# Moving eight modulation blocks into the output projection, and reading and projecting one branch's operands by token chunks

## The chip, the cores and the metric

The kernel runs on one core of a Trainium2 chip. A core has a matmul engine (TensorE, PE in the profile), a vector engine (VectorE, DVE), an activation engine (ScalarE, ACT), a general engine (GpSimd, POOL) and an engine that mostly issues transfers (SyncE, SP). Each engine takes its own instructions strictly in order; engines wait for one another through semaphores. 16 DMA engines move data between the large memory (HBM) and the on-chip memory. Matmuls write into accumulation banks (PSUM), which VectorE and ScalarE read. The metric is the device time of one execution in microseconds, lower is better.

## What is computed

One layer of a hybrid encoder in fp32, for 1024 prompt tokens and 64 sample tokens (2 sequences in all, D_MODEL = 1024). Both sequences share the weights and are laid side by side, 1088 tokens. Cut to what matters here:

```python
mod = jax.nn.silu(c) @ w_ada + b_ada                  # 6 x 1024 numbers for each sequence
sh1, sc1, g1, sh2, sc2, g2 = jnp.split(mod[:, None, :], 6, axis=-1)
u = _rmsnorm(x, norm1_g) * (1 + sc1) + sh1
proj = u @ w_in                                       # q, k, v, mLSTM operands, gates ga and gb
...
y_a = _stick_breaking(q, k, v)                        # scores, log-sigmoids, reverse cumsum, product with v
...
y_b = jax.nn.sigmoid(mo) * h                          # mLSTM branch
merged = jax.nn.sigmoid(ga) * (y_a @ w_a) + jax.nn.sigmoid(gb) * (y_b @ w_b)
x = x + g1 * (merged @ w_out)
u2 = _rmsnorm(x, norm2_g) * (1 + sc2) + sh2
x = x + g2 * ((silu(u2 @ w_ff_gate) * (u2 @ w_ff_up)) @ w_ff_down)
```

`g2` is the last of the six modulation vectors. Nothing reads it before the down projection of the feed-forward part.

## The kernel before

**Number format and tiles.** A matrix product in fp32 is made of three matmuls on pairs of reduced-precision parts, a high part and the rest (`mm3`, L76 to L78: high x high, high x low, low x high). Weight tiles come as a raw tile (`wr`, 512 KB, three buffers), which is turned into a high and a low part (`wh`, `wl`, three buffers each) by `w_unit` (L61); its load is L64. POOL makes these parts by default (L53 the high, L59 the low part), ACT and VectorE where the call says so (L47 and L56). D_MODEL is cut into 8 blocks of 128 (`KB` = 8). The 1088 tokens are cut into chunks of 320, 384 and 384 (`CHUNKS`), in the output projection into four quarters of 272. Long-lived activations are tiles of 128 x 1088 in a pool `up` of 16 slots: during the input projection these hold the normalised input (`uh0` to `uh7`, `ul0` to `ul7`), afterwards other tiles take the slots as they come free.

**What sets the order.** The program is written as generators that are drawn in turns (`run`, `chain`), and a scheduler of the compiler then fixes one order of instructions for each engine, by its own estimates of durations. On the chip nothing is reordered.

**Modulation blocks.** `ada_blocks` (L213) makes one block of 128 of the 6144 modulation numbers: a load of 512 KB of `w_ada` (L220), matmuls with the few columns of `c` (L223), a copy from the bank to the small tile `ada_sb` by VectorE (L226), a transpose on PE (L228), a sum and an addition of the bias. There are 48 blocks; blocks 40 to 47 are `g2`. Blocks 16 to 47 (`ada_left`) are filler, nearly all of them in the attention phase.

**The attention phase.** Four head pairs, `attention(0)` to `attention(3)`, each for two heads in turn. For each key tile: scores (`z`, L526 and L527), a mask, exponentials on ACT, a scan along the keys on VectorE (L396), a product (`be`, L397), transposes of that product on PE (named `ps_a<-ident,be`, L540), high and low parts (`ah` by ACT, `al` by VectorE, L56), and products with the values (`po`, L547). Matmuls of other work are put between, since the attention alone is a chain through four engines. In pairs 0 to 2 this filler is the gate units of the input projection (`gate_unit`, the last one `gb7`) and modulation blocks. In pair 3 it is the last eight modulation blocks and then `branch_b`.

**Branch b.** The mLSTM result has been put aside in HBM as ready high and low parts (`yb_d`). `load_y(4..7)` reads them into eight tiles `yh4` to `yh7`, `yl4` to `yl7` (L968), 544 KB each, into slots of the input tiles. `branch_b` then makes 8 output blocks `m` x 3 chunks `c`, chunks innermost, 12 matmuls each (`ps_b`). For each such unit the sigmoid gate `lgb` is read from HBM (L995), the sums are copied by ACT to `tb` (L997), multiplied by the gate on POOL (L998) and stored to `pb_d` (L999). `lgb` and `tb` share four small buffers. Between them `load_y(0..2)` reads three of the four stored attention outputs (`yr`, L971) and POOL makes their parts `yh0` to `yh2`, `yl0` to `yl2` (L53, L59); the fourth comes from pair 3 itself.

**Branch a and the output projection.** Branch a takes `yh0` to `yh3` through `w_a` (also named `ps_a`, now `ps_a<-yh`, L76), is gated, and added to branch b's result. Then the output projection's first half: for each `m` in 0 to 7, `wo_weights(m)` loads and converts `w_out`'s block (`wr_wo`, `wh_wo`, `wl_wo`) and reads the residual input (`xs`, 64 rows, through three buffers of the tag `dg`; `xr`), and `wo_half(m, 0)` makes two quarters with 24 matmuls each (`ps_wo`), with nine transposes of the residual input (`ps_xt`, L1105) into banks of `sbank`.

## Time and profile before

| | |
|---|---|
| three runs, us | 1793.95, 1791.36, 1785.57 (median 1791.36) |
| the profiled execution | 1789.02 us, of which 1787.1 us lie between its first and last instruction (the span) |
| mean granted clock of TensorE | 0.985 of full speed |
| busy: PE / VectorE / ScalarE / POOL | 1719.9 / 1050.1 / 741.3 / 547.1 us |
| the stretch that the change rewrites | 784.6 (end of `gb7`) to 899.1 us (first matmul of branch a) |
| the output projection's first half | from about 949 to 1003 us |

Times in all views are counted from the first instruction. A "busy" window says how long an engine had an instruction in work; the granted clock says which share of full speed the chip let TensorE have. A wait is shown in square brackets as the idle time of an engine just before an instruction, with the instruction of another engine (or the DMA) that ended it.

### The profile page before, as it was taken

How to read it: one execution, taken by the hardware profiler on the slowest of the kernel's cores; microseconds unless marked ns; L12 is line 12 of the kernel's file. 1: busy time of each engine (PE TensorE's matmuls, PEld its weight loads, DVE VectorE, ACT ScalarE, POOL GpSimd, SP SyncE). 2: the span in 40 equal slices, each digit the busy share in tenths (PEclk: the TensorE clock that was granted, in tenths of full speed). 3: DMA queues.
4: the chain of work that ended last, by engine and by line, in shares of the span. 5: the costliest groups of instructions: out<-in, count | busy, mean ns of one | idle time of the engine just before them, and what ended most of it. 6: DMA issues, size and time to landing. Idle time of an engine off the chain costs nothing. (4 is left out here: it accounts for less than half of the span.)

```text
span 1787.1 us, 32780 instructions
## 1 busy us (share of the span) xinstructions
PE 1719.9 (96%) x12670; PEld 1658.1 (93%) x12670; DVE 1050.1 (59%) x2030; ACT 741.3 (41%) x1506; POOL 547.1 (31%) x495
## 2 busy tenths in 40 slices
PE   5999999999999999988899999999999999999998
PEld 4799999999989988877899999999999999999998
DVE  6633415142346858696644289666555677667964
ACT  5333333324334535453523457433333355453444
POOL 2434544545343232224657250044322100001000
PEclk8999999999999999998999999999999999999999
DMA  9426566664386566586576345644433488899943
GB/s 269 123 64 212 129 218 138 197 162 141 122 213 144 142 147 156 137 245 195 179 231 202 99 141 161 196 158 148 144 108 98 147 243 236 290 343 340 295 151 101
DMA packets 359534, 320.25 MB, mean 179 GB/s; under 512 B 16727, under 2 KB 327507, under 8 KB 359379
## 3 DMA queue, kind: packets, MB, share of 16 engines
q1 hardware_dynamic: 345074, 270.77, 50.5%
q0 software_dynamic: 14304, 47.39, 10.7%
q8 instruction: 100, 1.64, 0.4%
q14 instruction: 56, 0.45, 0.1%
HBM read 241.01 MB, written 98.09 MB: 190 GB/s over the span
## 5 line engine op out<-in xcount | busy, mean ns | idle before, releaser
L1619 PE MATMUL ps_d<-o,wh_d 128*128 128x272 f32 x1232 | 230.8, 287 | 0.0
L1619 PEld LDWEIGHTS ps_d<-o,wh_d 128*128 128x128 f32 x1232 | 192.8, 188 | 0.0
L1619 PE MATMUL ps_d<-o,wl_d 128*128 128x272 f32 x616 | 176.4, 288 | 0.0
L1619 PEld LDWEIGHTS ps_d<-o,wl_d 128*128 128x128 f32 x616 | 115.5, 188 | 0.0
L47 ACT CAST w<-wr 128x512 fp32r<-128x512 f32 x140 | 85.0, 619 | 67.5 <-PE ps_gc L1392 22.0
L396 DVE TENSOR_TENSOR_SCAN re<-re 128x128 f32<-128x128 f32 (+3 forms) x64 | 103.3, 1615 | 14.8 <-ACT re L392 14.4
L56 DVE TENSOR_TENSOR w<-wr,w 128x512 fp32r<-128x512 f32 x140 | 94.6, 688 | 21.4 <-ACT w L47 19.2
L1603 POOL DMA_DIRECT2D dsum_d<-wr_d x12 | 6.5, 540 | 237.7 <-DVE wr_d L1601 221.2
L392 ACT ACTIVATE re<-z 128x512 f32<-128x512 f32 (+2 forms) x96 | 47.5, 495 | 72.7 <-DVE z L388 54.2
L1392 PE MATMUL ps_ga<-b1h,w 128*128 128x272 f32 x352 | 74.6, 289 | 3.0 <-ACT g L1377 1.8
L1392 PE MATMUL ps_gc<-b5h,w 128*128 128x272 f32 x352 | 75.2, 293 | 0.0
L1392 PE MATMUL ps_gd<-b7h,w 128*128 128x272 f32 x352 | 74.2, 290 | 0.2 <-DVE hst L1384 0.2
L1392 PE MATMUL ps_gb<-b6h,w 128*128 128x272 f32 x352 | 74.3, 289 | 0.0
L1392 PE MATMUL ps_gd<-b4h,w 128*128 128x272 f32 x352 | 74.0, 290 | 0.3 <-DVE hst L1374 0.2
L1392 PE MATMUL ps_gc<-b3h,w 128*128 128x272 f32 x352 | 73.7, 289 | 0.0
L1392 PE MATMUL ps_ga<-b2h,w 128*128 128x272 f32 x352 | 73.7, 288 | 0.0
L47 ACT CAST o<-hr 128x544 fp32r<-128x544 f32 x77 | 48.9, 645 | 51.0 <-DMA hr<-h_d 27.3
L47 ACT CAST wh_d<-wr_d 128x1024 fp32r<-128x1024 f32 (+1 forms) x42 | 41.1, 980 | 67.6 <-PE ps_d L1619 31.9
L76 PE MATMUL ps_ga<-uh,wh_ga 128*128 128x384 f32 (+1 forms) x192 | 64.6, 336 | 3.5 <-ACT gt_ga L825 3.4
L56 DVE TENSOR_TENSOR o<-hr,o 128x544 fp32r<-128x544 f32 x77 | 53.8, 720 | 20.7 <-ACT o L47 20.4
L56 DVE TENSOR_TENSOR al<-ps_a,ah 128x512 fp32r<-128x512 f32 (+1 forms) x80 | 49.5, 631 | 25.8 <-ACT ah L47 25.4
L76 PE MATMUL ps_gb<-uh,wh_gb 128*128 128x384 f32 (+1 forms) x192 | 64.6, 336 | 0.0
(552 smaller groups left out, 5884.8 us busy)
## 6 DMA issues: line engine op xcount, KB each, us to landing
wada<-in_w_ada SPq DMA_DIRECT2D x48, 512.0 KB
wr<-wsum_d SPq DMA_DIRECT2D x80, 256.0 KB
wr_d<-in_w_ff_down SPq DMA_DIRECT2D x34, 512.0 KB
h_d<-hst SPq DMA_DIRECT2D x44, 272.0 KB
wr<-in_w_ff_gate SPq DMA_DIRECT2D x40, 256.0 KB
hr<-h_d SPq DMA_DIRECT2D x33, 272.0 KB
wsum_d<-in_w_ff_up POOLq DMA_DIRECT2D x6, 1282.0 KB, 7.7
wsum_d<-in_w_ff_gate POOLq DMA_DIRECT2D x6, 1282.0 KB, 8.0
```

What stands on the lines that cost most here:

```text
L47: nc.scalar.copy(out, in_)
L56: nc.vector.tensor_sub(out, in_, h.bitcast(F32))
L76: nc.tensor.matmul(ps, wh, xh, start=first, stop=False)
L392: nc.scalar.activation(rest[:, c0 : c0 + w], ps, AF.Sigmoid, scale=-scale)
L396: nc.vector.tensor_tensor_scan(r, r, r, 1.0, ALU.mult, ALU.bypass)
L1392: nc.tensor.matmul(ps, w[:, a, j, :], b[j // 2][:, j % 2, :], start=p in (1, 6, 5, 7) and j == 0 and k == 0, stop=j == 3 and k == 2, skip_ ...
L1603: nc.gpsimd.dma_start(dsum_d[p][mp, ks[0] // 4][:, : P * n], flat)
L1619: nc.tensor.matmul(ps, a[:, j, mi, :], b[:, h], start=p not in (2, 4) and k == ks[0] and i == 0, stop=k == ks[-1] and i == 2, skip_group_c ...
```

## The change

Four things are changed.

1. Modulation blocks 40 to 47 leave pair 3's filler. Each is now made after one block of the output projection's first half, with a bank from `sbank`, its raw weights in a `wr` buffer and its small tile in a `dg` buffer, in place of `ada`'s own.
2. The last gate unit `gb7` makes its first chunk alone and the other two in turns, one eighth of the inner dimension at a time.
3. Branch b's operands are read by token chunks: 24 loads of 160 or 192 KB in place of 8 of 544 KB, the first chunk of all eight tiles first.
4. `branch_b` makes four output blocks for one chunk before the next chunk, and loads two pairs of weights at a time; the three reads of attention outputs come at other places of this order.

```diff
@@ -210,11 +210,11 @@
     C_s = xpool.tile([P, 4, 129], F32, tag="C_s", name="C_s", bufs=1)
     p0 = open_phase("start")
 
-    def ada_blocks(blocks, tag, nb, load):
+    def ada_blocks(blocks, tag, nb, load, new_bank=None, new_small=None):
 
         n = len(blocks)
         i0, step = blocks[0], blocks[-1] - blocks[0]
-        ps = bank(tag, f"ps_ada{i0}", nb)
+        ps = (new_bank or (lambda name: bank(tag, name, nb)))(f"ps_ada{i0}")
         for b, i in enumerate(blocks):
             raw = load(i)
             nc.sync.dma_start(raw, cols(w_ada, i * P))
@@ -222,7 +222,7 @@
                 g = 32 * (kb % 4)
                 nc.tensor.matmul(ps[g : g + 32, b * P : (b + 1) * P], cT[:, kb, :], raw[:, kb, :],
                                  start=kb < 4, stop=kb >= 4, tile_position=(0, g))
-        sb = small([P, n * P], f"ada_sb{i0}", "adas")
+        sb = (new_small or (lambda name: small([P, n * P], name, "adas")))(f"ada_sb{i0}")
         nc.vector.tensor_copy(sb, ps[:, 0 : n * P])
         for b in range(n):
             nc.tensor.transpose(ps[:, 256 + b * P : 256 + (b + 1) * P], sb[:, b * P : (b + 1) * P], ident)
@@ -343,15 +343,26 @@
     def evac_v(p, ps, s, e):
         nc.scalar.copy(pairs[p].vf[:, s:e], ps[:, : e - s])
 
-    def unit(name, fills, evac, alloc=None):
+    def unit(name, fills, evac, alloc=None, last=False):
+
         wh, wl = w_unit(fills, name)
         if alloc:
             alloc()
         for c, (s, e) in enumerate(CHUNKS):
+            if last and c:
+                break
             ps = bank("d", f"ps_{name}_{c}", cur["d"])
             for kb in range(KB):
                 mm3(ps[:, : e - s], wh[:, kb, :], wl[:, kb, :], uh[kb][:, s:e], ul[kb][:, s:e], kb == 0, kb == KB - 1)
             evac(ps, s, e)
+            yield
+        if last:
+            pss = [bank("d", f"ps_{name}_{c}", cur["d"]) for c in (1, 2)]
+            for kb in range(KB):
+                for ps, (s, e) in zip(pss, CHUNKS[1:]):
+                    mm3(ps[:, : e - s], wh[:, kb, :], wl[:, kb, :], uh[kb][:, s:e], ul[kb][:, s:e], kb == 0, kb == KB - 1)
+            for ps, (s, e) in zip(pss, CHUNKS[1:]):
+                evac(ps, s, e)
             yield
 
     def w_cols(c0):
@@ -824,7 +835,7 @@
             t = small([P, 384], f"gt_{name}{b}_{s}", "gt", bufs=cur["gt"])
             nc.scalar.activation(t[:, : e - s], ps[:, : e - s], AF.Sigmoid)
             nc.sync.dma_start(dst[b][:, s:e], t[:, : e - s])
-        return unit(f"{name}{b}", w_cols(c0 + b * P), fin)
+        return unit(f"{name}{b}", w_cols(c0 + b * P), fin, None, name == "gb" and b == KB - 1)
 
     def in_unit(name, c0, i, evac, alloc):
         return unit(name, w_cols(c0), lambda ps, s, e: evac(*i, ps, s, e), lambda: alloc(*i))
@@ -963,10 +974,6 @@
 
     def load_y(b):
         y_tiles(b)
-        if b >= 4:
-            for i, t in enumerate((yh[b], yl[b])):
-                nc.sync.dma_start(t.bitcast(F32), yb_d[b - 4, i])
-            return
         raw = up.tile([P, T], F32, tag="u", name=f"yr{b}")
         nc.sync.dma_start(raw, ya_d[b])
         for s, e in CHUNKS:
@@ -981,12 +988,14 @@
 
     def branch_b():
 
-        for m in range(KB):
-            if m % 2 == 0:
-                wh, wl = wb0 if m == 0 else wide_unit(w_b, 0, 4, m // 2, f"wb{m}")
-            if 2 <= m < 5:
-                load_y(m - 2)
-            for c, (s, e) in enumerate(CHUNKS):
+        left = 3
+        for m4 in range(0, KB, 4):
+            wbs = [wb0 if m == 0 else wide_unit(w_b, 0, 4, m // 2, f"wb{m}") for m in (m4, m4 + 2)]
+            for i, (c, m) in enumerate((c, m4 + i) for c in range(3) for i in range(4)):
+                (s, e), (wh, wl) = CHUNKS[c], wbs[m % 4 // 2]
+                if left and (m4 or i >= 6) and i % 3 == 0:
+                    load_y(3 - left)
+                    left -= 1
                 n = e - s
                 ps = bank("d", f"ps_b{m}_{c}", cur["d"])
                 for k in range(4):
@@ -1009,8 +1018,12 @@
         run(attention(p), chain(fill), 27, 0)
     wb0 = wide_unit(w_b, 0, 4, 0, "wb0")
     for b in range(4, 8):
-        load_y(b)
-    run(attention(3), chain(ada_left[24:32] + [branch_b()]), 27, 0)
+        y_tiles(b)
+    for s, e in CHUNKS:
+        for b in range(4, 8):
+            for i, t in enumerate((yh[b], yl[b])):
+                nc.sync.dma_start(t[:, s:e].bitcast(F32), yb_d[b - 4, i, :, s:e])
+    run(attention(3), branch_b(), 27, 0)
     ph.close()
 
 
@@ -1253,6 +1266,9 @@
     for m in range(KB):
         kept[m], xr = wo_weights(m)
         sqs = wo_half(m, 0, kept[m], m == 0, m == KB - 1, lambda i: None, xr)
+
+        ada_blocks((40 + m,), None, None, lambda i: wp.tile([P, KB, P], F32, tag="wr", name=f"wada{i}"), sbank,
+                   lambda name: npl.tile([P, P], F32, tag="dg", name=name, bufs=3))
     for p in order:
         op_tiles(0, p, order.index(p) < 4)
     rows2 = [npl.tile([P, HT], F32, tag="rr", name=f"rr{h}", bufs=1).rearrange("p (i t) -> p i t", i=2) for h in range(2)]
```

The compiled order of the two programs differs only from the last gate unit on. Three places show how.

TensorE, around the first matmuls of branch b (`ps_b0_0`). Before, they stand behind the last of the modulation blocks (`ps_ada46`, `ps_ada47`; `ps_ck` belongs to the sample's keys in pair 3):

```order
L463 MATMUL ps_ck3_8602<-ident_66,craw_k3_8600 128x128 x4
L228 MATMUL ps_ada46_9031<-ident_66,ada_sb46_9042 128x128
L547 MATMUL po3_0_3_8545<-ah_3_0_3_6_8589,vs3_0_8323 128x256
L547 MATMUL po3_0_3_8545<-al_3_0_3_6_8590,vs3_0_8323 128x256
L547 MATMUL po3_0_3_8545<-ah_3_0_3_6_8589,vs3_0_8323 128x128
L547 MATMUL po3_0_3_8545<-al_3_0_3_6_8590,vs3_0_8323 128x128
L228 MATMUL ps_ada47_9047<-ident_66,ada_sb47_9058 128x128
L76 MATMUL ps_b0_0_9063<-yh4_8304,wh_wb0_8300 128x320
L77 MATMUL ps_b0_0_9063<-yl4_8305,wh_wb0_8300 128x320
```

In the changed program (its lines are 11 higher here):

```order
L551 MATMUL ps_a2_1_3_6_7786<-ident_66,be_2_1_7_7737 128x128 x2
L228 MATMUL ps_ada39_8281<-ident_66,ada_sb39_8292 128x128
L558 MATMUL po2_1_3_7746<-ah_2_1_3_4_7778,vs2_1_7210 128x256
L558 MATMUL po2_1_3_7746<-al_2_1_3_4_7779,vs2_1_7210 128x256
L558 MATMUL po2_1_3_7746<-ah_2_1_3_4_7778,vs2_1_7210 128x256
L558 MATMUL po2_1_3_7746<-al_2_1_3_4_7779,vs2_1_7210 128x256
L551 MATMUL ps_a3_0_0_0_8389<-ident_66,be_3_0_0_8370 128x128
L551 MATMUL ps_a3_0_0_0_8389<-ident_66,be_3_0_1_8381 128x128 x2
L76 MATMUL ps_b0_0_8957<-yh4_8304,wh_wb0_8300 128x320
L77 MATMUL ps_b0_0_8957<-yl4_8305,wh_wb0_8300 128x320
```

Branch b's first matmul has moved from the end of pair 3's first head to its beginning, where pair 2 (`po2`) is still at its last products; its place on PE is 111 rows earlier.

TensorE, at the end of pair 3. Before, the last products of the attention (`po3_1_3`) are followed by the last two units of branch b, 24 matmuls, of which the first three are shown, and then by branch a:

```order
L547 MATMUL po3_1_3_8878<-ah_3_1_3_6_8922,vs3_1_8334 128x256
L547 MATMUL po3_1_3_8878<-al_3_1_3_6_8923,vs3_1_8334 128x256
L547 MATMUL po3_1_3_8878<-ah_3_1_3_6_8922,vs3_1_8334 128x128
L547 MATMUL po3_1_3_8878<-al_3_1_3_6_8923,vs3_1_8334 128x128
L76 MATMUL ps_b7_1_9529<-yh4_8304,wh_wb6_9449 128x384
L77 MATMUL ps_b7_1_9529<-yl4_8305,wh_wb6_9449 128x384
L78 MATMUL ps_b7_1_9529<-yh4_8304,wl_wb6_9450 128x384
```

In the changed program the last unit of branch b (`ps_b7_2`) stands 46 attention instructions earlier, directly behind the pair's last scores, and the same place reads:

```order
L558 MATMUL po3_1_3_8894<-ah_3_1_3_4_8926,vs3_1_8350 128x256
L558 MATMUL po3_1_3_8894<-al_3_1_3_4_8927,vs3_1_8350 128x256
L558 MATMUL po3_1_3_8894<-ah_3_1_3_6_8938,vs3_1_8350 128x256
L558 MATMUL po3_1_3_8894<-al_3_1_3_6_8939,vs3_1_8350 128x256
L558 MATMUL po3_1_3_8894<-ah_3_1_3_6_8938,vs3_1_8350 128x128
L558 MATMUL po3_1_3_8894<-al_3_1_3_6_8939,vs3_1_8350 128x128
L76 MATMUL ps_a0_0_9517<-yh0_9071,wh_wa0_9503 128x320
L77 MATMUL ps_a0_0_9517<-yl0_9072,wh_wa0_9503 128x320
```

Branch a (`ps_a0_0<-yh0`) now follows the attention's last products directly.

SyncE, in the middle of the output projection's first half (`wr_wo6` and `wr_wo7` are raw weights, `xs` and `xr` residual inputs, `x1_d` stores of the result, `wr_wp0` the weights of a later part). Before:

```order
L64 DMA wr_wo6_10684<-in_w_out 128x8x128
L1043 DMA xs4_10508<-in_x_sample 64x128
L1143 DMA x1_d_10166<-x1_0_0_0_10167 128x544
L64 DMA wr_wo7_10770<-in_w_out 128x8x128
L1043 DMA xs5_10594<-in_x_sample 64x128
L1045 DMA xr3_10424<-in_x_prompt 128x8x128
L1045 DMA xr4_10510<-in_x_prompt 128x8x128
L1143 DMA x1_d_10166<-x1_0_1_0_10169 128x544
L1271 DMA wr_wp0_11107<-in_w_out 128x8x128
L1043 DMA xs6_10680<-in_x_sample 64x128
```

In the changed program:

```order
L220 DMA wada45_10649<-in_w_ada 128x8x128
L64 DMA wr_wo6_10668<-in_w_out 128x8x128
L1058 DMA xr5_10564<-in_x_prompt 128x8x128
L1058 DMA xr6_10666<-in_x_prompt 128x8x128
L1156 DMA x1_d_10054<-x1_0_0_1_10056 128x544
L220 DMA wada46_10751<-in_w_ada 128x8x128
L1056 DMA xs5_10562<-in_x_sample 64x128
L64 DMA wr_wo7_10770<-in_w_out 128x8x128
L1156 DMA x1_d_10054<-x1_0_0_1_10056 128x544
L220 DMA wada47_10851<-in_w_ada 128x8x128
L1056 DMA xs6_10664<-in_x_sample 64x128
```

The loads of `w_out` now alternate with loads of `w_ada`, and block 6's sample input (`xs6`) stands behind the last of them.

## Rows read from the trace of the kernel before

**Rows 1.** From the profile's page: TensorE's busy tenths in 40 equal slices of the span (about 45 us each; 9 is 90% or more).

```profile
PE   5999999999999999988899999999999999999998
```

**Rows 2.** Busy time by window: the window in us, its length, then for PE, PE's weight loads, VectorE, ACT and POOL the busy us and the number of instructions, then TensorE's granted clock, the busy share of the DMA engines and GB/s. The whole rewritten stretch first, then pieces of it, then one of the output projection.

```profile
784.60:899.10 114.50, 100.86 (x721) 89.84 (x721) 79.03 (x149) 54.34 (x124) 54.19 (x48) 0.93 0.70 214
790.00:796.00 6.00, 5.62 (x50) 4.61 (x49) 6.00 (x22) 4.63 (x10) 0.56 (x1) 1.00 1.03 380
802.00:808.00 6.00, 2.59 (x19) 1.68 (x21) 5.11 (x6) 2.43 (x5) 0.00 (x0) 0.69 1.16 320
880.00:886.00 6.00, 3.17 (x24) 2.90 (x22) 2.33 (x4) 1.81 (x4) 6.00 (x7) 1.00 0.23 73
963.00:970.00 7.00, 7.00 (x58) 6.79 (x57) 1.03 (x3) 1.96 (x6) 5.56 (x6) 1.00 1.09 315
```

**Rows 3.** Who ended PE's idle time from 784.6 to 899.2 us: the waiting group, what it waited for, us in total, times, the longest.

```profile
PE ps_b L76 <- ACT tb L997: 4.4, 2, 2.8
PE ps_ada L223 <- DMA wada<-in_w_ada: 3.4, 1, 3.4
PE ps_ada L228 <- DVE ada_sb L226: 2.1, 1, 2.1
PE po L547 <- DVE al L56: 1.4, 1, 1.4
PE ps_a L540 <- DVE be L397: 1.2, 2, 0.7
PE po_s L499 <- DVE al_s L56: 0.8, 1, 0.8
PE z L526 <- ACT be L393: 0.4, 1, 0.4
```

**Rows 4.** PE in order of time, in pair 3's first head: start, us, line, output and inputs, shape, count. A modulation block, the product behind it, and branch b's first matmul.

```profile
823.08 0.65 PE L223 MATMUL ps_ada<-wada,cT 128*32 128x128 f32 x16
823.66 0.39 PE L547 MATMUL po<-ah,vs 128*128 128x256 f32 x1
...
827.39 0.38 PE L76 MATMUL ps_b<-yh,wh_wb 128*128 128x320 f32 x1
```

**Rows 5.** SyncE's DMA issues in order of time (start, us that the issues took, line, transfer): branch b's operands, the modulation weights behind them, and one read of an attention output.

```profile
783.98 0.43 SPq L968 DMA_DIRECT2D yh<-yb_d  x1
784.50 0.40 SPq L968 DMA_DIRECT2D yl<-yb_d  x1
...
789.13 0.32 SPq L968 DMA_DIRECT2D yl<-yb_d  x1
...
795.11 8.92 SPq L220 DMA_DIRECT2D wada<-in_w_ada  x3
...
863.20 0.50 SPq L971 DMA_DIRECT2D yr<-ya_d  x1
```

**Rows 6.** PE in order of time, later: the last scores of pair 3, two products of its end, the first branch-b matmul behind the last product, branch a's first matmul, and the residual transposes that begin in two successive blocks of the output projection.

```profile
870.65 0.40 PE L527 MATMUL z<-kl,qs 128*128 128x512 f32 x1
...
890.69 0.28 PE L547 MATMUL po<-al,vs 128*128 128x256 f32 x1
890.81 0.28 PE L547 MATMUL po<-ah,vs 128*128 128x256 f32 x1
...
894.90 0.39 PE L76 MATMUL ps_b<-yh,wh_wb 128*128 128x384 f32 x1
...
899.11 0.31 PE L76 MATMUL ps_a<-yh,wh_wa 128*128 128x320 f32 x1
...
962.15 0.27 PE L1105 MATMUL ps_xt<-ident,xs 64*128 64x64 f32 x1
...
969.38 0.27 PE L1105 MATMUL ps_xt<-ident,xs 64*128 64x64 f32 x1
```

**Rows 7.** VectorE in order of time: a scan over 1024 keys in pair 2, the same in pair 3, and the product behind it. In brackets the idle time before, and who ended it.

```profile
780.29 2.29 DVE L396 TENSOR_TENSOR_SCAN re<-re 128x1024 f32<-128x1024 f32 x1 [0.61 <-ACT re L392]
...
875.14 3.12 DVE L396 TENSOR_TENSOR_SCAN re<-re 128x1024 f32<-128x1024 f32 x1 [0.67 <-ACT re L392]
878.36 1.23 DVE L397 TENSOR_TENSOR be<-be,re 128x1024 f32<-128x1024 f32 x1
```

**Rows 8.** POOL's groups from 866 to 900 us: line, operation, output and inputs, shape, count, then busy us, mean ns of one, and the idle time before them with what ended it.

```profile
L998 POOL TENSOR_TENSOR tb<-tb,lgb 128x384 f32<-128x384 f32 (+1 forms) x9 | 10.1, 1120 | 7.8 <-ACT tb L997 3.0 <-ACT ah L47 2.3 <-DMA lgb<-gb_d 1.7
L59 POOL TENSOR_TENSOR yl<-yr,yh 128x384 fp32r<-128x384 f32 (+1 forms) x9 | 9.4, 1074 | 0.7 <-PE ps_b L77 0.7
L53 POOL TENSOR_SCALAR yh<-yr 128x384 fp32r<-128x384 f32 (+1 forms) x9 | 8.9, 1013 | 1.0 <-DMA yr<-ya_d 1.0
```

**Rows 9.** POOL in order of time: the high parts of three attention outputs, the low parts of the first, and the two parts of a weight tile of the output projection.

```profile
868.22 3.12 POOL L53 TENSOR_SCALAR yh<-yr 128x320 fp32r<-128x320 f32 x3 [1.01 <-DMA yr<-ya_d]
871.30 3.84 POOL L59 TENSOR_TENSOR yl<-yr,yh 128x320 fp32r<-128x320 f32 x3
...
876.08 4.36 POOL L53 TENSOR_SCALAR yh<-yr 128x320 fp32r<-128x320 f32 x3
...
885.89 1.42 POOL L53 TENSOR_SCALAR yh<-yr 128x320 fp32r<-128x320 f32 x3
...
976.64 1.05 POOL L53 TENSOR_SCALAR wh_wo<-wr_wo 128x1024 fp32r<-128x1024 f32 x1 [2.23 <-PE ps_wo L77]
977.77 2.40 POOL L59 TENSOR_TENSOR wl_wo<-wr_wo,wh_wo 128x1024 fp32r<-128x1024 f32 x1
```

## Prediction

> **What bounds the kernel now.** I read the slices of the span first: TensorE (PE) is at nine tenths or more almost everywhere, and dips in those from about 760 to 985 us [rows 1]. So the kernel is bound by PE's work, and a change can win only where PE waits or runs slowly, or by removing work. This one removes none. Next I read windows of the stretch that it rewrites, from the last input matmul (784.6) to branch a's first matmul (899.1): 114.5 us, PE busy 100.86, granted clock 0.93 [rows 2]. That gives two recoverable amounts: 114.5 - 100.9 = 13.6 us idle, and about (1 - 0.93) x 100.9 = 7.1 us that matmuls lost at the lower of the clock's two levels (1.2 of 2.4 GHz). **20.7 us** is all that can be had here. Then I asked who ended the idle time [rows 3]: 3.4 and 2.1 us are modulation blocks (a load, then VectorE's copy), 1.4, 1.2, 0.8 and 0.4 are the attention's own chain, and 4.4 us, late, are branch b's evacuations. The early part is a queue effect. PE runs in order, and branch b's first matmul (827.39) stands behind all eight modulation blocks [rows 4], whose loads SyncE issued in two groups, the first from 795.11 [rows 5]. Branch b's operands had been requested by 789.13, so PE had 47 us of useful matmuls that it could not reach. Meanwhile VectorE was nearly full (6.00 and 5.11 us of 6), PE was busy only 2.59 us of 6 in the second of these windows, and the clock fell to 0.69 there [rows 2].
>
> **The modulation blocks.** One block is 16 matmul records, 0.58 us from its first to the next work (823.08 to 823.66) [rows 4], and a transpose, for which I take 0.12 us, the spacing of a small attention matmul [rows 6]: 0.7 us, 5.6 for eight. Leaving attention(3) saves 5.6; in the output projection PE is busy 7.00 of 7 us [rows 2], nothing hides them, and they cost 5.6. The move is worth zero by itself. Their VectorE work is covered there (1.03 of 7 us busy). Each transpose now waits for VectorE's copy of that block. In the new order six transposes stand 18 or more output matmuls behind their block, one stands 4 behind and one directly behind: I take 1 us in all (bounds 0 and 2, the 2.1 us of rows 3).
>
> **The head of attention(3).** The new order puts the first branch-b matmul directly behind the last two transposes that stayed, 45 PE instructions after the last input unit, and spreads branch b from there to the end. All idle time of rows 3 before the last scores can be filled. Not all of it will be. Branch b's results pass through four small buffers (gate load, ACT copy, POOL product, store), and where this loop was late in the kernel before, PE waited 2.8 us at once [rows 3]. The new order has a denser run of such units between the two heads. I take 3.5 us of idle left here (bounds 1.5, about the attention waits of 1.4, and 6). The chunked operand loads can decide only their start: the three chunks bring the same bytes, and by the chip's program order each first-chunk load still waits until the last input chunk has read the tile that it overwrites, which interleaving the last two chunks brings forward by six matmuls, about 1 us. That edit and the turns are worth 0 to 1 us; I take 0.
>
> A load of 544 KB took 5.0 us from issue to its first reader (863.20 to 868.22) [rows 5, 9], and the issues of such loads stand 0.5 us apart (783.98, 784.50). The Trainium skill, DMA: Bandwidth & Descriptors, section Bandwidth, advises against this edit: batch transfers to 1 MiB or more; its section on the anatomy of one DMA gives some 2.0 us fixed for each. Estimated from that page, eight loads paid one behind another would take 8 x 2.4 = 19 us, and the first branch-b matmul would come some 13 us late, the whole at 1803. The issues 0.5 us apart say that such loads overlap, so it is no bound here.
>
> **The tail of attention(3).** This is what the change adds. Before, 24 branch-b matmuls (894.90 to 899.11) stood behind the last attention matmul, and more lay between [rows 6]. In the new order the last branch-b unit stands directly behind the last scores, and 46 attention matmuls follow with nothing between, then branch a. PE's work from the last scores on is 12 x 0.175 + 46 x 0.12 = 7.6 us; the time is set by two chains. First, the attention: from the last scores (870.65) to the end of the product after the scan (878.36 + 1.23) are 9 us [rows 6, 7]; four groups follow, each of transposes, ACT's high part, VectorE's low part and products, about 2 us each (an estimate: two such evacuations, 0.5 us of matmuls and the hops between), so 17 us. Second, POOL: it turns three stored attention outputs into branch a's operands. In the new order the first of these loads stands behind the store of branch-b unit (4, 2), 24 branch-b matmuls and some 30 others (8 us) before the end of the scores; with copy, product, issue and the 5.0 us of landing (some 7 us), POOL starts about 1 us before that end. It then has to do 9 high parts, 7 low parts and 3 products before branch a can run: at the mean rows 9 x 1.01 + 7 x 1.07 + 3 x 1.12 = 20 us [rows 8], so branch a starts 19 us after the last scores. With the high parts as beside a quiet VectorE (1.42 us for three) POOL's sum is 15 us; with both parts as beside a busy one (4.36 and 3.84 for three) 25.5 [rows 9]. I take 19: idle 19 - 7.6 = **11.4 us**, bounds 9 (the attention's 17 us) and 17 (POOL's 25.5).
>
> POOL's three high parts took 4.36 us beside VectorE and 1.42 at 885.89; the scan took 3.12 us at 875.14 and 2.29 us at 780.29 [rows 7, 9]. The Trainium skill, SBUF — State Buffer, section Who interferes with whom, says that a VectorE instruction with two SBUF inputs and a GpSimd one that reads SBUF share a port as an exclusive lock. By that rule the two chains of the tail would add wherever they meet, which is rival B. The scan lost 0.8 us of 3.1, not all of it, so the trace bears out a part.
>
> PE is then sparse for 19 us. Before, the two sparse places (2.59 and 3.17 busy of 6 us [rows 2]) cost the 7.1 us together. I take 3 us lost to the clock (bounds 1 and 5).
>
> **The weights of the output projection.** One block takes 7.2 us (962.15 to 969.38) [rows 6]. Before, its raw weights came up to three blocks ahead; now modulation loads take every second of the three raw buffers, and on SyncE a modulation load that waits for a weight conversion or for PE stands in front of the next weight load and the sample inputs. From the buffer's release: issue 0.4, landing up to 5.0, conversion 1.05 + 2.40 [rows 5, 9], 8.9 us, against some 7 to 8 us of PE work that the new order leaves for blocks 5 to 7 and 15 for the earlier ones. I take 2 us (bounds 0 and 5).
>
> **The sum.** The 20.7 us go; 3.5 + 11.4 + 3 = 17.9 come in the stretch: 2.8 us won. The output projection gives back 1 + 2 = 3 (the 5.6 cancel). Net **+0.2 us**: 1789.0 in terms of the profiled run (1789.02, a span of 1787.1 and 1.9 around it), which lies 2.3 us under the median of the three runs, 1791.36. I put 1790. With all bounds at the good end: -20.7 + 1.5 + 9 + 1 + 0 = -9.2; at the bad end: -20.7 + 6 + 17 + 5 + 2 + 5 = +14.3, of which not all can come true together.
>
> **The rivals.** *A, the stretch closes up:* branch b fills the head and the tail is only as long as PE and a quiet POOL make it (14 us, idle 6.4), with 1.5 idle before, 1 lost to the clock and 1 given back later: -10.8, 1778 to 1780. For it: idle head time is the plainest loss in the profile. Against it: no filler stands in the new tail. *B, slower, the tail's two chains hinder each other:* POOL's high parts tripled beside VectorE and the scan lost 0.8 us beside POOL [rows 7, 9]; if each waits for the other throughout, the attention's 17 and POOL's quiet 14 us add up, branch a starts 31 us after the last scores, idle 23.4 instead of 11.4: +12, 1801. It decides from about 28 us on. For it: POOL was full (6.00 of 6) in 880 to 886 [rows 2]. Against it: ACT and PE have a share of the attention's 17. *C, slower, the weights run dry:* blocks 5, 6 and 7 each wait 4 us (half of the 8.9): 12 instead of 2, +10, 1800. Against it: 15 us of slack for the earlier ones. *D, the edit of the loads does not do what it says:* the pieces start when the whole tiles did, eight issues take 4 us, and since all share the DMA engines a piece lands after twice the 5.0 us: 14 us, against some 8 of PE work before the first branch-b matmul. 6 us late: 1796. For it: the wait for the tiles' last readers stays.
>
> **How the numbers follow.** Forecast as summed 0.50, A 0.22, B 0.12, C 0.07, D 0.09. A measurement of this kernel tells from no change about 0.5%, 9 us. A is faster but for its upper edge; of the forecast's own spread (1784 to 1797) nothing is beyond 9 us; B and C lie beyond the bound, and with them a part of the forecast's bad end. Faster 0.21, same 0.58, slower 0.21. The range leaves out the lower half of A and the upper part of B and C, no more than 2 in 10: 1780 to 1801.
>
> **What would show it.** The first branch-b matmul within 8 us of the last input matmul, and no PE wait for a modulation load, show the head right. A PE idle time of 9 us or more between the last scores and branch a, ended by POOL or VectorE and followed by slow matmuls, shows the tail right; branch a under 15 us after the last scores shows A. In the output projection: eight blocks of 0.7 us more, waits for weight conversions in blocks 5 to 7 of 0 to 5 us together. I am wrong if the tail holds no such gap, or if a wait appears that is not listed here.

## The result: slower by 0.5%

| | before | changed |
|---|---|---|
| median, us (10 runs each) | 1789.80 | 1800.03 |
| changed / before, 95% interval | | 1.0050 [1.0038, 1.0063] |
| profiled run, us (its span) | 1789.02 (1787.1) | 1801.31 (1799.6) |

The forecast was 1790, no change. 10 us came instead, just inside the range and on its bad side. One of the ten changed runs, 1845.37 us at a granted clock of 0.889, is left out of the ratio.

First the changed kernel's windows, with the columns of [rows 2]: the rewritten stretch, from the last input matmul to branch a; its two parts, divided 0.4 us behind the start of the last scores; two pairs of pieces; the output projection; the feed-forward part up to the down projection.

```profile
788.45:895.86 107.41, 93.77 (x585) 87.89 (x584) 75.89 (x126) 55.06 (x125) 55.85 (x50) 0.91 0.67 198
788.45:877.49 89.04, 81.43 (x528) 77.28 (x527) 61.49 (x111) 47.99 (x112) 37.48 (x31) 0.94 0.71 211
877.49:895.86 18.37, 12.35 (x58) 10.62 (x58) 14.40 (x16) 7.07 (x15) 18.37 (x20) 0.74 0.46 135
812.00:818.00 6.00, 2.28 (x13) 1.39 (x13) 5.50 (x7) 2.83 (x6) 5.92 (x3) 1.00 0.62 226
818.00:824.00 6.00, 5.06 (x17) 4.97 (x18) 4.65 (x5) 2.21 (x5) 1.61 (x3) 0.50 0.63 203
882.00:888.00 6.00, 1.35 (x5) 0.93 (x5) 6.00 (x4) 0.60 (x2) 6.00 (x5) 0.85 0.76 222
888.00:894.00 6.00, 5.55 (x23) 4.71 (x22) 3.29 (x6) 2.41 (x5) 6.00 (x8) 0.50 0.18 59
943.60:1068.60 125.00, 119.86 (x1014) 113.91 (x1013) 52.98 (x101) 47.73 (x105) 54.22 (x41) 0.99 0.51 145
1068.60:1547.05 478.45, 474.36 (x3735) 472.22 (x3734) 324.43 (x656) 204.48 (x395) 87.51 (x80) 0.99 0.56 166
```

The same for the last two in the kernel before:

```profile
948.80:1061.70 112.90, 111.76 (x878) 109.47 (x877) 57.23 (x90) 50.64 (x111) 59.88 (x45) 0.98 0.44 131
1061.70:1535.95 474.25, 471.89 (x3732) 470.46 (x3733) 322.05 (x648) 203.59 (x393) 83.46 (x79) 1.00 0.56 168
```

The stretch is 7.1 us shorter than before (114.5, [rows 2]), but no better filled: 13.6 us idle as before, and (1 - 0.91) x 93.8 = 8.4 us lost to the clock in place of 7.1. It is shorter only because the blocks' matmuls are gone. The output projection is 12.1 us longer: 8.1 busy, the rest idle. The feed-forward part behind it is 4.2 us longer as well. From branch a's first matmul to the output projection's are 47.7 us in place of 49.7. The first 784 us, the same program in both, differ by 4 us in these two profiles and in others by up to 8; that is the spread of single runs, so the verdicts below rest on ratios of many runs, and a profile only says where a wait is.

Who ended PE's idle time in the changed kernel, from 785 to 900 us (columns as [rows 3]):

```profile
PE po L558 <- DVE al L56: 4.7, 1, 4.7
PE ps_b L76 <- ACT tb L1006: 3.3, 2, 3.1
PE ps_a L551 <- DVE be L408: 3.0, 3, 2.2
PE ps_a L551 <- DMA pb_d<-tb: 1.5, 1, 1.5
PE po L558 <- ACT ah L47: 0.9, 1, 0.9
```

and from 943 to 1080 us:

```profile
PE ps_wo L78 <- POOL wl_wo L59: 2.1, 1, 2.1
PE ps_xt L1118 <- DMA xs<-in_x_sample: 2.1, 1, 2.1
PE ps_gb L1408 <- DVE w L56: 1.2, 1, 1.2
PE ps_ada L228 <- DVE ada_sb L226: 0.4, 1, 0.4
PE ps_wo L76 <- POOL wh_wo L53: 0.3, 1, 0.3
```

The waits on modulation loads and on `ada_sb` of [rows 3] are gone from the stretch, as meant. In their place PE waits on VectorE's `al` in the tail and on ACT's `tb` in the head, and after each of the two waits the clock is at the lower level: 0.50 in 818 to 824 and in 888 to 894, right behind six-microsecond pieces with 2.28 and 1.35 us of PE work.

**The head**, SyncE's issues:

```profile
782.22 0.34 SPq L1025 DMA_DIRECT2D yh<-yb_d  x1
...
803.37 0.32 SPq L1025 DMA_DIRECT2D yl<-yb_d  x1
803.88 0.32 SPq L1004 DMA_DIRECT2D lgb<-gb_d  x1
804.44 0.94 SPq L64 DMA_DIRECT2D wr_wb<-in_w_b  x2
```

and POOL behind them:

```profile
808.26 0.88 POOL L1007 TENSOR_TENSOR tb<-tb,lgb 128x320 f32<-128x320 f32 x1 [3.42 <-ACT re L403]
...
812.81 3.95 POOL L59 TENSOR_TENSOR wl_wb<-wr_wb,wh_wb 128x1024 fp32r<-128x1024 f32 x1
816.72 1.70 POOL L1007 TENSOR_TENSOR tb<-tb,lgb 128x320 f32<-128x320 f32 x1
```

The 24 chunk loads fill SyncE's queue for 21 us. The first gate load (issued at 791.83 in the kernel before) and a weight load wait behind them, POOL's first product starts at 808.26, and the second stands behind that weight's conversion. With four buffers for gates and sums, branch b can't go on. Another 2.2 us of PE's idle time in the head, a wait for `be` at 790.98, stand behind a scan that took 5.43 us, where one in pair 2 took 2.29 [rows 7]; POOL worked beside it, on `wl_wb` until 787.44, and the scan ended 2.15 us later, at 789.59:

```profile
784.16 5.43 DVE L407 TENSOR_TENSOR_SCAN re<-re 128x1024 f32<-128x1024 f32 x1 [0.61 <-ACT re L403]
```

**The tail**, VectorE, then POOL beside it, then PE:

```profile
881.43 2.01 DVE L56 TENSOR_TENSOR wl_wa<-wr_wa,wh_wa 128x1024 fp32r<-128x1024 f32 x1
883.36 3.07 DVE L407 TENSOR_TENSOR_SCAN re<-re 128x1024 f32<-128x1024 f32 x1
886.36 0.53 DVE L56 TENSOR_TENSOR al<-ps_a,ah 128x384 fp32r<-128x384 f32 x1
```

```profile
882.32 1.97 POOL L59 TENSOR_TENSOR yl<-yr,yh 128x384 fp32r<-128x384 f32 x1
884.26 2.43 POOL L53 TENSOR_SCALAR yh<-yr 128x320 fp32r<-128x320 f32 x1
```

```profile
877.09 0.40 PE L538 MATMUL z<-kl,qs 128*128 128x512 f32 x1
...
886.94 0.58 PE L558 MATMUL po<-al,vs 128*128 128x256 f32 x1 [4.65 <-DVE al L56]
...
895.86 0.57 PE L76 MATMUL ps_a<-yh,wh_wa 128*128 128x320 f32 x1
```

Branch a starts 18.8 us after the last scores; 19 was forecast. VectorE runs without a pause here, and a weight of branch a, not needed for long, stands in front of the last scan. POOL's last part that branch a's first unit reads (`yl`, 894.78 to 895.66) came just as late.

**A block in the output projection**, PE:

```profile
963.45 0.29 PE L76 MATMUL ps_wo<-mh,wh_wo 128*128 128x272 f32 x1
963.67 0.65 PE L223 MATMUL ps_ada<-wada,cT 128*32 128x128 f32 x16
964.25 0.39 PE L77 MATMUL ps_wo<-ml,wh_wo 128*128 128x272 f32 x1
964.48 0.29 PE L78 MATMUL ps_wo<-mh,wl_wo 128*128 128x272 f32 x1
```

From the first row's output matmul to the last row's, two places further in that work, are 1.03 us; matmuls two places apart start 0.25 apart where nothing stands between. So a block takes 0.78 us: 0.58 for its 16 matmuls and 0.20 in gaps on either side of them. Its transpose adds 0.11 (956.96 to 957.32 are 0.36 us for two places). That is 0.9 us, not 0.7, and by the busy time, 8.1 us for eight, 1.0.

**The sample input** in the output projection, SyncE:

```profile
963.37 0.37 SPq L220 DMA_DIRECT2D wada<-in_w_ada  x1
...
964.41 0.43 SPq L64 DMA_DIRECT2D wr_wo<-in_w_out  x1
964.89 1.28 SPq L1056 DMA_DIRECT2D xs<-in_x_sample  x1
```

PE waits for this load of 64 rows until 971.89 (2.1 us of the list above). It is queued behind two loads of 512 KB.

### The profile page after: what moved, and what is told of

Its sections match the earlier page's. It is cut to its first block, busy times and chain, and to the rows that moved or that the text cites. A ratio compares the mean times of both kernels' runs of the same rounds, so it can differ in the third digit from the quotient of the medians.

```text
span 1799.6 us, 32781 instructions
## 1 busy us (share of the span) xinstructions
PE 1725.6 (96%) x12670; PEld 1666.9 (93%) x12670; DVE 1049.6 (58%) x2030; ACT 741.4 (41%) x1506; POOL 547.4 (30%) x495
## 3 DMA queue, kind: packets, MB, share of 16 engines
q0 software_dynamic: 14304, 47.39, 10.6%
## 5 line engine op out<-in xcount | busy, mean ns | idle before, releaser
L407 DVE TENSOR_TENSOR_SCAN re<-re 128x128 f32<-128x128 f32 (+3 forms) x64 | 106.3, 1662 | 16.0 <-ACT re L403 15.6
L403 ACT ACTIVATE re<-z 128x512 f32<-128x512 f32 (+2 forms) x96 | 47.4, 495 | 64.8 <-DVE z L399 48.8
```

The source lines that it names most:

```text
L403: nc.scalar.activation(rest[:, c0 : c0 + w], ps, AF.Sigmoid, scale=-scale)
L407: nc.vector.tensor_tensor_scan(r, r, r, 1.0, ALU.mult, ALU.bypass)
```

## The experiments

Five rounds each, ratios to runs of the kernel before on the same chip. A difference of two ratios is given in us of 1790.

| run | median | ratio, 95% interval |
|---|---|---|
| e1 blocks back at the head of pair 3 | 1790.84 | 1.0005 [0.9988, 1.0021] |
| e2 only the blocks moved | 1801.35 | 1.0068 [1.0048, 1.0089] |
| e3 blocks behind branch b in pair 3 | 1791.56 | 1.0009 [0.9993, 1.0024] |
| e4 blocks with raw buffers of their own | 1795.36 | 1.0037 [1.0018, 1.0055] |
| e5 gate load ahead of late chunks | 1797.95 | 1.0052 [1.0035, 1.0069] |
| e6 = e5 and e3 | 1789.87 | 1.0007 [0.9991, 1.0023] |
| e7 changed, no blocks | 1782.13 | 0.9965 [0.9954, 0.9976] |
| e8 = e5 and e4 | 1794.53 | 1.0029 [1.0018, 1.0041] |
| e9 late chunks requested by POOL | 1803.75 | 1.0074 [1.0055, 1.0093] |
| e10 = e9 and e3 | 1795.59 | 1.0021 [1.0006, 1.0036] |
| e11 = e9, blocks spread | 1789.82 | 0.9991 [0.9978, 1.0005] |
| e12 a weight's low part left out | 1800.12 | 1.0047 [1.0029, 1.0066] |
| e13 changed, blocks spread | 1787.06 | 0.9977 [0.9961, 0.9994] |
| e14 before, blocks spread | 1788.57 | 0.9988 [0.9973, 1.0003] |
| e15 before, no blocks | 1786.68 | 0.9978 [0.9965, 0.9990] |
| e16 six of the eight blocks | 1802.36 | 1.0068 [1.0048, 1.0089] |
| e17 blocks spread more densely | 1791.36 | 0.9993 [0.9977, 1.0010] |

### Which part of the change is it? (e1 to e4)

Theory P: where the blocks are. Theory L: the chunk loads and the new order of branch b.

e1, the blocks go back, the rest stays:

```diff
-    run(attention(3), branch_b(), 27, 0)
+    run(attention(3), chain(ada_left[24:32] + [branch_b()]), 27, 0)
...
-        ada_blocks((40 + m,), None, None, ...
```

> The change with its first part undone: the eight modulation blocks are filler ahead of branch b in pair 3 again, the chunked loads, the turns and the new order of branch b stay. Theory P (the placement of the eight blocks makes the loss: in the output projection they cost their full work and some 5 us of waits, and in pair 3 idle time takes their place): back to the kernel before, ratio 0.998 to 1.001, perhaps 2 us faster by branch a. Theory L (the loss comes from the chunked loads and the chunk-wise order of branch b): the loss stays, ratio 1.003 to 1.006.

e2 is the opposite: the kernel before with only the new `ada_blocks` call and the filler `branch_b()`.

> The kernel before with the first part alone: the eight blocks in the output projection's first half, all else as before. Theory P: slower as the full change, ratio 1.003 to 1.007, with 4 to 6 us of PE waits in the output projection (for sample inputs behind SyncE and for a low weight part). Theory L: no loss, ratio 0.998 to 1.001, since the blocks only change places.

e3, the blocks as the last filler of pair 3:

```diff
+    run(attention(3), chain([branch_b()] + ada_left[24:32]), 27, 0)
```

> The change, but the eight blocks are filler of pair 3 behind branch b, and none is in the output projection. In its compiled order they stand in the bare tail, between the last scores and branch a. Theory P: the tail's idle time (6 us) and most of its slow clock (4 us) are filled with the blocks, and the output projection is as before: 1780 to 1785 us, ratio 0.994 to 0.998. Rival W (the tail is set by VectorE's queue and the blocks' copies and loads only lengthen it): branch a starts 4 us or more later than in the change, ratio 0.999 to 1.003.

e4, raw weights and small tiles of the blocks from other tags:

```diff
-        ada_blocks((40 + m,), None, None, lambda i: wp.tile([P, KB, P], F32, tag="wr", ...
+        ada_blocks((40 + m,), None, None, lambda i: up.tile([P, T], F32, tag="u", ...
```

> The change, but in the output projection the raw modulation weights go into free slots of the activation pool and the small tile into another buffer set, so that weights, sample inputs and modulation blocks share no buffers. Theory P: the 4.9 us of waits there go, 1794 to 1796 us, ratio to before 1.001 to 1.004. Rival D (the waits come from the transfers themselves, not from the buffers): 2 us or more of the waits stay, ratio 1.004 to 1.006.

By its interval e1 can't be told from the kernel before, nor e2 from the changed one: the blocks' place makes the loss, and no other part of the change shows in the total. The chunk loads do what they were meant for: in e2, without them, PE waits 1.2 us for branch b's operands (`yh<-yb_d`), in the changed kernel not at all. e3 brings nothing over e1: branch a starts 24.3 us after the last scores in place of 18.8, as rival W had it. In e4 the waits on `xs`, `wl_wo` and `wh_wo` are gone, one of 2.2 us for a modulation load takes their place, and the output projection takes 119.0 us: so the shared buffers made those waits. In the total the 2.3 us between the two ratios lie within their intervals, and this profile, of 1790.67 us, is the fastest of e4's twelve runs.

### The head's wait (e5, e6, e8, e9, e10)

e5 requests the chunks 1 and 2 inside `branch_b`:

```diff
+                if not m4 and i in (2, 5):
+                    load_yb(1 + i // 5)
...
-    for s, e in CHUNKS:
+    load_yb(0)
```

> The changed kernel, but branch b's operands of the second and third chunk are requested inside branch_b (before its third and sixth unit), so that the first gate load no longer stands behind all 24 chunk loads on SyncE. Theory H (the full queue on SyncE makes the first gate load, and with it the first POOL product and the third branch-b unit, late): the PE wait on tb of 3.1 us at about 819 us falls under 1 us, the slow clock behind it (817.9 to 824.8) goes, and the kernel takes 1794 to 1797, 1.002 to 1.004 of before. Rival Q (POOL's order, a weight conversion ahead of the second product, makes it late): the wait of some 3 us stays, 1798 to 1801. By both the output projection stays as it is, some 12 us longer than before.

> As the run before, and the eight modulation blocks stand behind branch b in the filler of attention pair 3, none in the output projection. If placement of the blocks is the loss (P) and the late gate loads are a second one (H): the output projection falls back to 113 us, the stretch from the last input matmul to branch a keeps no wait on tb over 1 us and takes 106 to 110, and the kernel takes 1784 to 1788, 0.997 to 0.999 of before. If the blocks in the tail only swap places with other waits, as when they were put last without the earlier gates: 1790 to 1792, 1.000 to 1.001.

> The earlier chunk requests of the first run of this group, with the blocks in the output projection on raw and small buffers of their own kind (the 16 wide slots and another tag). If the gains of both edits add (about 4 us each): 1790 to 1793, 1.000 to 1.002 of before, with PE waits of at most 2.5 us in the output projection. If the earlier gates bring nothing: 1795 as with own buffers alone, 1.003 to 1.004.

In e5 the first gate load goes out at 787.3, but the compiled order still puts the second one and the weight load behind all chunks (802.0 and 800.2), and the wait on `tb` is 2.9 us. By their intervals e5 can't be told from the changed kernel, e8 not from e4, e6 not from e3. So e9 takes those loads off SyncE altogether:

```diff
-                nc.sync.dma_start(t[:, s:e].bitcast(F32), ...
+                (nc.gpsimd if s else nc.sync).dma_start(t[:, s:e].bitcast(F32), ...
```

> The changed kernel, but the second and third chunks of branch b's operands are requested by POOL, which is idle there for about 14 us; SyncE keeps the first chunk only. In the compiled order the first gate load then stands behind 8 chunk loads in place of 24, and the first two POOL products stand ahead of the weight conversion. Theory H2 (the gate and weight loads queued behind the chunk loads on SyncE make the head's wait): no PE wait on tb over 1 us, no slow clock at 818 to 825, the stretch from the last input matmul to branch a 101 to 104 us in place of 107.7, 1794 to 1797. Rival: what makes the wait is the rate of the loop of four small buffers itself, or the POOL requests cost what they save: 106 to 109 us, 1799 to 1801.

> As the run before, with the eight modulation blocks behind branch b in the filler of attention pair 3 and none in the output projection. By theory H2 (4 us won in the head) and P (the blocks cost some 9 us less here than in the output projection): 1784 to 1788, 0.997 to 0.999 of before. If the head gives nothing: 1790, 1.000.

In e9 POOL's second product starts 24.7 us behind the last input matmul (787.25 to 811.91) in place of 28.6, and the wait on `tb` is gone (0.2 us in place of 3.3). So H2 had its cause right. But PE waits 6.1 us more for `al`, `be` and `ah` (14.7 in place of 8.6), and the stretch takes 109.1 us in place of 107.4. The largest of these waits, 3.9 us for `al` at 798.92, is a new one of another kind. In this compiled order VectorE has the cast of the sample's queries in front of that `al`, and their load has not landed:

```profile
798.08 0.20 DVE L487 CAST zq<-qs 128x64 fp32r<-128x64 f32 x1 [3.71 <-DMA qs<-qk_d]
```

So e9 doesn't show what the wait on `tb` is worth by itself. Besides, POOL spends 0.55 us on each of the 16 requests; e11 and e13, which differ only in who makes them, are 2.5 us apart (0.9991 and 0.9977), less than their intervals can tell. e10 is no better than e3, either.

### What the blocks cost in each place (e7, e15)

> The changed kernel with the eight modulation blocks left out altogether (g2 isn't computed, its numbers are set to 0), so the feed-forward result isn't added. It gives the whole price of the blocks in the output projection. Theory P (their loads share buffers and SyncE's queue with the weights): the output projection falls from 125 to 112 to 114 us, with no PE wait on xs or wl_wo over 0.5 us, the start of the feed-forward part gets back 1 to 2 us: 1785 to 1788, 12 to 15 us under the changed kernel, of which 8 are the blocks' own matmuls. Rival W (their work alone): the waits on xs and wl_wo stay at about 4 us, only 8 us go: 1791 to 1793.

> The kernel before without its eight blocks in pair 3 (g2 isn't computed, its numbers are set to 0). If the blocks cost their own work where they stood (the prediction's step, 5.6 us, by the later rows 8): 1781 to 1784, equal to the changed kernel without blocks. If they cost more there because of their two waits (3.4 and 2.1 us): 1776 to 1780, and the chunked loads and turns lose 3 to 5 us. If they were nearly free there: 1786 to 1789, and these edits win 4 to 6 us without the blocks.

The blocks cost 0.9978 to 1, **3.9 us** (1.8 to 6.3 by the interval), where they stood, and 0.9965 to 1.0050, **15.2 us** (about 12 to 18 by the two intervals), in the output projection. Without them the other edits win 2.3 us (0.9978 to 0.9965, less than the intervals can tell). -3.9 - 2.3 + 15.2 = +9.0 is the result, as it must be, since the three differences share their runs. The blocks' work is some 8 us in either place: 8.1 more busy in the output projection, and 100.86 x 0.93 - 93.77 x 0.91 = 8.5 us at full speed less in the stretch. The windows show why it was cheap before; the stretch of e15:

```profile
788.66:899.41 110.75, 96.73 (x586) 88.64 (x586) 79.14 (x126) 54.59 (x124) 54.89 (x51) 0.89 0.65 200
```

Eight blocks fewer, but 14.0 us idle and (1 - 0.89) x 96.7 = 10.6 lost to the clock, in place of 13.6 and 7.1: the blocks had been keeping PE busy in time that attention leaves open. Without them PE waits 12.5 us for the attention's own chain, where it waited 3.8 [rows 3]:

```profile
PE ps_a L541 <- DVE be L398: 3.9, 2, 2.2
PE po L548 <- DVE al L56: 3.1, 3, 1.4
PE po L548 <- ACT ah L47: 2.8, 2, 2.1
PE ps_a L541 <- DVE al L56: 2.7, 1, 2.7
```

In e7 the output projection is

```profile
942.43:1053.74 111.31, 110.19 (x878) 107.87 (x877) 53.55 (x84) 48.97 (x108) 57.38 (x43) 1.00 0.43 127
```

with 1.1 us idle, all at its end, as in the kernel before (a wait for VectorE's `x` as the feed-forward part begins). So there each block is added whole, and waits with it: 5.1 us idle in place of 1.1. Between the profiles of e7 and of the changed kernel lie 13.7 us in the output projection, 2.9 in the feed-forward part and -1.0 in the stretch: 15.6, against 15.2 by the ratios.

### The tail's chain (e12)

```diff
-        was = [wide_unit(w_a, 0, 4, m // 2, f"wa{m}", hi_act, lo_dve) for m in (m4, m4 + 2)]
+        was = [wide_unit(w_a, 0, 4, m // 2, f"wa{m}", hi_act, (lambda *_: None) if m == 4 else lo_dve) for m in (m4, m4 + 2)]
```

The matmuls read the high part in its place.

> The changed kernel without the low part of one weight tile of branch a (the third pair of blocks): its conversion on VectorE is left out and the matmuls read the high part in its place, so the numbers of two output blocks lose precision. The order of everything else is the same. Theory V (in the tail, VectorE's queue is the chain: this conversion stands in front of the last scan while that scan's input is ready): the scan starts 2.0 us earlier, PE's wait on al falls from 4.7 to 2.7 us, branch a starts 16.5 to 17 us after the last scores in place of 18.8, 1798. Rival (POOL's operand parts set branch a's start, as forecast): branch a stays at 18.5 to 19 us after the last scores, and the idle time moves to a wait on POOL.

```profile
880.90 3.08 DVE L407 TENSOR_TENSOR_SCAN re<-re 128x1024 f32<-128x1024 f32 x1
883.90 0.53 DVE L56 TENSOR_TENSOR al<-ps_a,ah 128x384 fp32r<-128x384 f32 x1
```

PE's wait falls from 4.7 to 2.7, and branch a starts 16.4 us after the last scores (876.55 to 892.91). So VectorE's queue set that start. POOL stood close behind it: in e12 its last part for branch a's first unit ends at 894.17, 1.5 us earlier than in the changed kernel, and the third low-part matmul of branch a starts 0.39 us behind the one before it (893.84, 894.23), where 0.14 is the usual distance. The total doesn't tell: 2.4 us are 0.13%, and the interval is wider; the output projection takes 128.7 us in this profile (its waits 6.3 us in place of 5.1, the clock at 0.96). Whether the gain is given back there each time or lies in the spread of single runs isn't settled.

### The feed-forward part (e16)

> The changed kernel without the last two of its eight blocks in the output projection (a quarter of g2 isn't computed, set to 0). Theory F (the last blocks hold raw buffers, POOL and VectorE when the feed-forward part's first weights are made): its first 10 us lose nothing against the kernels without blocks there, the feed-forward part takes 474 to 476 us in place of 478.5, and the output projection 2 to 3 us less: 1793 to 1796. Rival: any block there delays them: only the two blocks' 2 us go, 1797 to 1799.

Theory F falls: with two blocks fewer it is no faster. PE waits 4.2 us for VectorE's `x` as the feed-forward part begins, 1.1 in the kernel before. In the changed kernel and in e3, two windows each, 45 to 30 us ahead of the first feed-forward matmul and the 15 us behind it:

```profile
1023.60:1038.60 15.00, 15.00 (x120) 14.15 (x119) 6.23 (x19) 5.45 (x11) 4.61 (x4) 0.89 0.51 152
...
1068.60:1083.60 15.00, 13.75 (x92) 13.47 (x91) 11.88 (x29) 7.75 (x15) 3.83 (x2) 0.77 0.72 196
```

```profile
1014.70:1029.70 15.00, 15.00 (x118) 14.70 (x117) 10.57 (x12) 11.40 (x23) 4.76 (x2) 0.99 0.25 79
...
1059.70:1074.70 15.00, 15.00 (x109) 14.63 (x110) 7.85 (x21) 8.19 (x16) 0.05 (x1) 0.89 0.78 211
```

With blocks there, VectorE (third pair of numbers) is busy 4.3 us less in the first window and 4.0 us more after the start, where it still makes four low parts of the operands (`b3l`, `b4l`, `b6l`, `b7l`); in e3 it makes none there. PE gets 13.75 x 0.77 = 10.6 us of full-speed work done in the first 15, against 13.4. Why the compiled order does these operands later, in kernels with eight and with six blocks, stays open.

### Spread blocks (e11, e13, e14, e17)

```diff
+    def mixed():
+        blocks = iter(ada_left[24:32])
+        for n, _ in enumerate(branch_b()):
+            yield
+            if n % 3 == 1:
+                yield from next(blocks)
+    run(attention(3), mixed(), 27, 0)
```

e11 has this on e9, e13 on the changed kernel, e14 on the kernel before; e17 is e13 with `n % 2 == 1 and n < 16`.

> As the run before, but a modulation block is put behind every third unit of branch b, so that each has time for its load. If the blocks lost time for their late loads at the end (a wait of 4.0 us on the last one): their cost falls to their own 8 to 8.5 us and the kernel takes 1783 to 1787, 0.996 to 0.998 of before. If the tail's idle time was hiding part of the blocks: equal to the run before or up to 3 us slower.

> The changed kernel with a modulation block behind every third unit of branch b, none in the output projection, and the chunk loads on SyncE as changed. If the chunk loads on POOL cost 2 to 4 us by themselves: 1784 to 1787, 0.996 to 0.998 of before, a version that beats both. If they cost nothing where blocks are spread: 1789 to 1790, 0.999 to 1.000.

> The kernel before with its eight blocks spread behind every third unit of its own branch b (whole-tile loads, chunks innermost) and nothing else changed. If the chunked loads and turns are worth nothing (theory P): the same as the changed kernel with spread blocks, within 0.15%, 1784 to 1788. If they are worth something once the blocks stand well: 3 to 6 us slower than that one, 1788 to 1791.

> The changed kernel with a modulation block behind every second unit of branch b from the second to the sixteenth, none in the output projection and none left for the tail. If the wait of 4.1 us for a modulation load is a pure loss of the late last blocks: it goes, 1782 to 1785, 0.995 to 0.997 of before. If the blocks at the end only filled time in which the attention's chain keeps PE idle anyway: 1787 to 1789, 0.998 to 0.999, with a longer wait for VectorE in the tail; if the loads then come in too dense a row (issue behind gate loads and stores on SyncE), waits for modulation loads of 3 us or more in the head and 1789 to 1791.

e13 is the fastest complete kernel, 0.23% under before; its interval ends at 0.9994, and it can't be told from e14, so the chunks aren't shown to have a share in it. The intervals of the other three spread runs, e11, e14 and e17, reach beyond 1. The stretch of e13:

```profile
790.07:899.70 109.63, 97.85 (x722) 87.94 (x722) 78.59 (x148) 54.34 (x126) 53.24 (x52) 0.97 0.75 221
```

All eight blocks are in it, and it loses 11.8 us idle and 2.9 to the clock, 14.7 in place of 20.7. A wait of 4.1 us for one modulation load is left. e17 doesn't win it back: with no block left for the tail, waits for VectorE and a load (3.2 us) come elsewhere, and by its interval it can be told neither from e13 nor from the kernel before.

## Why the prediction was wrong, point by point

**What bounds the kernel, and the 20.7 us.** Right as a reading; wrong as a sum that an order can collect. Branch b's matmuls were indeed moved forward, and the waits for modulation blocks went, but 13.6 + 8.4 = 22.0 us were lost in the stretch after the change, not 17.9. e15 shows the reason: take the blocks away, and PE comes sooner to the next link of the attention's chain, and waits there.

**The modulation blocks.** "Leaving attention(3) saves 5.6; ... and they cost 5.6. The move is worth zero by itself" is **the step that failed**. e2, which makes this move alone, costs 12.2 us (8.6 to 15.9). The term that was mis-sized is the price in the output projection: 15.2 in place of 5.6. What they saved, 3.9, can't be told from 5.6. Three things were mis-sized or missing: 0.7 us of work is 0.9 to 1.0 us (the gaps beside the 16 matmuls); work in a stretch that waits for a chain hides in it, so that removing some 8 us of it gave back about a half; and the price in the output projection has two parts behind it, below. One part was over-priced: the transposes' waits for VectorE's copies, 0.4 us in place of 1.

**The head.** 3.5 us of idle were taken; 89.04 - 81.43 = 7.6 came, outside the bounds: 3.3 behind `tb`, 2.8 behind `be` and 1.5 at one group of transposes. The first branch-b matmul stood 10.9 us behind the last input matmul (788.14 to 799.03), where 8 was the sign. The loop of four buffers was named as the danger and was it, through a cause that was not seen: the issues of the chunk loads. "Worth 0 to 1 us" for that edit isn't contradicted by the total (e1: 1.0005, an interval of 5.9 us), though it made a new wait. The estimate of 1803 from the Trainium skill, DMA: Bandwidth & Descriptors, section Anatomy of one DMA — SWDGE (gpsimd) path, did not come: PE waits nowhere for these loads. That section gives its fixed time for loads that GpSimd issues; these went out from SyncE.

**The tail.** The start of branch a was right, 18.8 us for 19, and so was POOL's sum: its nine high parts, seven low parts and three products took 19.8 us (875.84 to 895.66) for 20, and began 1.25 us before the last scores for 1. But PE stood behind the other chain: e12 shows VectorE's queue in front, which was forecast at 17 us. That both ended at about the same time, and the number with them, is luck. Idle was 18.37 - 12.35 = 6.0 us, not 11.4, and under the 9 that was to show the tail right, since PE's work there took 12.35 us, much of it at half clock. The reading of the slow scan was wrong: it was said to lose "0.8 us of 3.1, not all of it". In the rows of the tail VectorE's weight part ends at 883.44, POOL's low part at 884.29, VectorE's scan at 886.43 and POOL's high part at 886.69: 0.85, 2.14 and 0.26 us apart, where the last three took 1.00, 2.29 and 0.47 at their quickest. So the two took turns, and each long duration is the wait for the other's instruction and then its own time. e12 repeats it: the scan ends at 883.98, and POOL's low part, begun at 881.79, at 884.77, 2.98 us in place of 1.00. The Trainium skill, SBUF — State Buffer, section Who interferes with whom, tells of an exclusive lock on a port that the two share, and this trace agrees. Rival B, by which the chains would add throughout, still didn't come: 18.8 us, not 31.

**The clock.** 3 us taken, bounds 1 and 5; (1 - 0.94) x 81.4 + (1 - 0.74) x 12.35 = 4.9 + 3.2 = 8.1 came. The tail's share was right; the head's, behind the wait on `tb`, was left out.

**The output projection.** 1 + 2 us of waits were taken, bounds 0 and 7; 4.0 us more idle came (5.1 in place of 1.1), within the bounds and at the places that were named (weights, and sample inputs behind modulation loads). The rest of the 12.1 us is the blocks' work, 8.1 busy against 5.6 forecast.

**What had no term.** The feed-forward part, 478.5 us in place of 474.3; the sum stopped at the end of the output projection. It is 477 to 481 us in every one of the profiles with blocks there (e2, e4, e5, e8, e9, e12, e16), 474 to 476 in those without. One gain was missed as well, the 2.0 us of branch a's stage: it takes 47.4 to 47.8 us in every profile without blocks in pair 3, and 48.5 to 50.9 in those with them.

So the sum missed by this much, in the two profiles: the stretch +1.3 us (4.1 more lost, 2.8 more of the blocks' work gone), the output projection +3.5, the feed-forward part +4.2, branch a's stage -2.0: 7.0 us in all, where the ratios' interval is 6.8 to 11.3 us. The rest of the 12.5 us between the two spans lies ahead of the stretch (3.9) and in the down projection (1.4).

## What to carry to other kernels

Work was cheap here where PE waits for a chain (3.9 us) and cost its full length and more where PE is full (15.2), so price moved work by the stage it goes to and by the one it leaves, each with the work left out, before adding up. Idle time between the links of a chain wasn't collected here by moving one piece of filler; spreading it through the stretch came nearest, and held the clock up (0.97 in place of 0.93). Look at what stands behind a row of small loads in its issuing queue: here a gate load went out 12 us later.

## What the runs showed of the hardware that was not expected

- Behind waits of 1.5 and 3.1 us, and behind one of 4.7 us, the clock fell, and stayed low while PE was busy again: with 2.28 and 1.35 us of work in six, it was at 0.50, the lower of its levels (1.2 of 2.4 GHz), in the next six, with PE busy 5.06 and 5.55 us. Half of 5.55 us is 2.8 us lost behind a wait of 4.7.
- 16 small fp32 matmuls between output matmuls cost 0.20 us beyond their own 0.58.
- A load of 64 rows, issued at 964.89 behind two of 512 KB with the DMA engines near full (0.90 busy from 963.6 to 973.6), reached its reader at 971.89.
- A scan that took 2.29 us in pair 2 took 3.07 and 5.43 us beside POOL's work, and a high part of POOL's 2.43 us beside the scan, 0.47 at its quickest: VectorE and POOL took turns by whole instructions.
